# A transformer layer's two attentions: fill matmuls in pieces of six behind groups of transposes, and another order of units, loads and buffers

## The chip, the cores and the metric

The kernel runs on one core of a Trainium2 chip. The metric is the device time of one execution in microseconds (us); a kernel's time is the median of its runs. The core has five engines that run their own instruction streams in order and wait for each other through semaphores: TensorE (PE: matrix products and transposes), VectorE (DVE), ScalarE (ACT), GpSimd (POOL) and SyncE (SP), which here only issues DMA transfers. ACT issues some transfers too, in its own stream between its other work.

## The reference, cut to what matters

One layer of an encoder over 2048 tokens of 1024 features, in float32:

```
h  = rms_norm(x, norm_mix);  z = h @ w_in
z  -> q_A | k_A | v_A | q_B | k_B | v_B | gate_A | gate_B
yA = windowed GQA: 8 heads in 2 key groups, blocks of 128 queries, |t-s| <= 128,
     ALiBi slopes, a sink logit per head
yB = neighbourhood attention, 8 heads: each token of a 32 x 64 grid sees 8 rows x 16 columns,
     with a learned relative bias (rpb)
merged = sigmoid(gate_A) * (yA @ w_proj_a) + sigmoid(gate_B) * (yB @ w_proj_b)
x  = x + merged @ w_out
x  = x + relu(rms_norm(x) @ w_up)^2 @ w_down;   out = rms_norm(x)
```

## The kernel before, in words

Every float32 operand of a matmul is split into a rounded part and a remainder, and a product is made of three matmuls (`mm3`, L201: high by high, high by low, low by high), each 128x512. The stages run one after the other: the norm and the input projection (to about 535 us), attention A (to about 830 us), attention B (to about 1171 us), then the second projection, `w_out` and the MLP. This change touches only the two attentions; the streams of the later stages are the same in both kernels.

**Attention A** (`attn_a`, L829) has 32 units, one for each key group `g` and block `i` of 128 queries. A unit has two halves. The first makes the scores: for each of four heads two matmuls into a PSUM tile `s` (L844/845; three such tiles take turns), bias and maximum on DVE (L846), exponential on ACT (L853), sums on DVE, and the normalisation on POOL (L857). The second half has three groups (two at the ends of the sequence). A group is four PE transposes into a PSUM tile `pt` (L863; two such tiles), a rounded copy on ACT (`ph`, L866), the remainder on DVE (`pl`, L867), and two matmuls that add to the PSUM tile `av` (L868/869). There is one `av` tile, so the next unit's first `av` matmul waits until ACT and DVE have taken the unit's result out into `ya` (L872/873).

**Attention B** (`attn_b`, L1011) has 32 units, 8 heads by 4 column tiles, of the same two halves: scores (L1029), bias and maximum on DVE into `sb`/`stb` (L1034), exponential (L1040), normalisation on POOL (L1045), then four groups of three or four transposes (L1057), `phb` (L1062), `plb` (L1063), and `av` matmuls (L1068); `yb` takes the result out (L1076/1077). The bias tables `biass` and `biasl` of a head are made on POOL (L997) from `braw` and from `masks`, which are loaded once (L979, 1.6 MB). A head's keys `kb` are 2 MB in three transfers (`load_k`, L1006 to 1008), a unit's queries `qb` 256 KB (L1016).

**The fill.** Both attentions have PE wait for other engines, so other matmuls stand between their parts: the gates of two token pages (`gate_tile`, 16 tiles, each with two runs of 24 matmuls into a PSUM tile `mm`, whose result `z` ACT stores to `zg`), and then, in attention B, the projection of `yA` (`proj_tile`, 8 tiles of 48 matmuls). The latter needs pages of `yA` that are loaded back from memory and split on ACT (L282) and DVE (L283), in `y_page`. `chain` runs these generators one after the other and starts the loads of weights two tiles ahead. `paced` says how early a piece of fill may stand: its n-th piece, a run of 24 (or, in a projection tile, of 48), is put with `tc.issue_after` behind the last `av` matmul of one unit, kept in `done`. That sets an order on PE only and makes no engine wait; Tile's scheduler makes the streams of the engines from it. `drive` runs the units, with the first halves two units ahead of the second.

**Buffers.** `pools` opens the SBUF buffers of a stage on the left or right side, in the order of its list. A buffer of attention B that lies where one of attention A lay can be loaded only when A's last reader is through: the list decides what a load waits for.

## Time and profile before

| | us |
|---|---|
| runs of the kernel before | 2677.56, 2681.48, 2682.59 |
| their median | 2681.48 |
| the profiled execution's own time | 2674.47 |
| its span in the profile | 2672.7 |
| PE busy in the span | 2578.7 (96%) |
| DVE, ACT, POOL busy | 1703.9, 1308.6, 335.3 |
| mean granted PE clock | 0.987 |

The rows of the profile have these forms. A window gives, for a stretch of time, each engine's busy time with the number of its instructions, the granted clock of PE as a share of full speed, the share of the DMA engines that is busy, and GB/s. A wait gives the instruction that stood, what released it, and the total, the number and the longest of such waits. A row of the timeline gives an instruction's start, its duration, its line and tiles, and in brackets the idle time of its engine just before it, with what ended it. A matmul's duration overlaps the next one's, so that two starts tell what one costs, and PE's busy time counts no moment twice. The span is 1.8 us shorter than the execution's own time, and that is 7.0 us shorter than the median of the three runs.

### The profile page before, as it was taken

The page shows a single profiled execution, that of the slowest core. Times are in us where ns is not written, and L with a number is a line of the kernel's source. Part 1 is how long each engine was busy: PE and PEld are TensorE (multiplying, and loading weights), DVE is VectorE, ACT ScalarE, POOL GpSimd, SP SyncE. Part 2 cuts the span into 40 slices and gives each one's busy share as a digit, 9 for nine tenths or more (in the row PEclk, how much of TensorE's full clock was granted, in tenths as well). Part 3 has the DMA queues.
Part 4 walks back from the last instruction along what each step waited for, and adds up shares of the span by engine and source line. Part 5 has one row for each costly group of instructions (what it writes and reads, how often), then busy time and mean ns, then how long its engine had stood idle before and what let it go on. Part 6 is the DMA issues. An engine that isn't in the chain of part 4 may idle for free. (4 is left out here: it accounts for less than half of the span.)

```text
span 2672.7 us, 34547 instructions
## 1 busy us (share of the span) xinstructions
PE 2578.7 (96%) x11936; PEld 2127.9 (80%) x11936; DVE 1703.9 (64%) x2700; ACT 1308.6 (49%) x2349; POOL 335.3 (13%) x460
## 2 busy tenths in 40 slices
PE   7999999989997989999999999999999999999998
PEld 6887888877876877888877888888887888888887
DVE  7756576646663566656597766776566634555667
ACT  7365465547664665532435555554444232332444
POOL 1001001033333644300000000000000000000011
PEclk9999999989998999999999999999999999999999
DMA  5778478873337798769798655864436935445555
GB/s 181 228 197 284 147 274 262 258 222 88 95 87 198 199 255 248 215 211 345 252 339 261 237 208 199 280 222 147 150 115 245 325 123 177 148 145 169 184 186 174
DMA packets 348159, 553.21 MB, mean 207 GB/s; under 512 B 30904, under 2 KB 152888, under 8 KB 345808
## 3 DMA queue, kind: packets, MB, share of 16 engines
q1 hardware_dynamic: 328912, 506.96, 58.9%
q10 hardware_dynamic: 15552, 32.51, 3.3%
q0 software_dynamic: 3520, 11.54, 1.2%
q8 instruction: 94, 1.54, 0.2%
q14 instruction: 81, 0.66, 0.1%
HBM read 364.19 MB, written 186.71 MB: 206 GB/s over the span
## 5 line engine op out<-in xcount | busy, mean ns | idle before, releaser
L287 PE MATMUL b<-dwh,dah 128*128 128x512 f32 x896 | 348.9, 389 | 0.4 <-DVE dwh L283 0.4
L288 PE MATMUL b<-dwh,dah 128*128 128x512 f32 x896 | 348.0, 389 | 0.0
L286 PE MATMUL b<-dwh,dah 128*128 128x512 f32 x896 | 338.5, 389 | 1.7 <-ACT dwh L282 1.7
L282 ACT CAST dah<-da 128x1024 fp32r<-128x1024 f32 (+1 forms) x128 | 120.8, 944 | 367.4 <-PE b L288 245.1
L286 PE MATMUL zb<-zh,zwhl 128*128 128x512 f32 x728 | 285.8, 393 | 7.9 <-ACT zb L532 2.4
L288 PE MATMUL zb<-zh,zwhl 128*128 128x512 f32 x728 | 283.8, 391 | 1.2 <-DVE zwhl L283 1.2
L287 PE MATMUL zb<-zh,zwhl 128*128 128x512 f32 x728 | 284.8, 391 | 0.0
L283 DVE TENSOR_TENSOR dah<-da,dah 128x1024 fp32r<-128x1024 f32 (+1 forms) x128 | 139.3, 1090 | 218.4 <-ACT dah L282 213.9
L286 PE MATMUL b<-ubh,uwhlb 128*128 128x512 f32 x592 | 231.7, 391 | 5.0 <-ACT uwhlb L282 3.4
L287 PE MATMUL b<-ubh,uwhlb 128*128 128x512 f32 x592 | 231.3, 391 | 0.0
L288 PE MATMUL b<-ubh,uwhlb 128*128 128x512 f32 x592 | 229.4, 390 | 0.0
L286 PEld LDWEIGHTS b<-dwh,dah 128*128 128x128 f32 x896 | 168.1, 188 | 36.9 <-ACT dwh L282 2.1
L287 PEld LDWEIGHTS b<-dwh,dah 128*128 128x128 f32 x896 | 168.2, 188 | 35.7 <-DVE dwh L283 0.8
L288 PEld LDWEIGHTS b<-dwh,dah 128*128 128x128 f32 x896 | 168.2, 188 | 34.9
L279 DVE TENSOR_TENSOR uc<-b,uc 128x512 f32<-128x512 f32 x160 | 109.3, 689 | 117.3 <-PE b L288 111.1
L286 PEld LDWEIGHTS zb<-zh,zwhl 128*128 128x128 f32 x728 | 136.7, 188 | 41.6 <-ACT zb L532 3.9
L288 PEld LDWEIGHTS zb<-zh,zwhl 128*128 128x128 f32 x728 | 136.8, 188 | 30.8 <-DVE zwhl L283 2.7
L287 PEld LDWEIGHTS zb<-zh,zwhl 128*128 128x128 f32 x728 | 136.8, 188 | 27.4
L202 PE MATMUL mm<-zh,whl 128*128 128x512 f32 x384 | 156.0, 406 | 0.6 <-ACT zh L282 0.6
L204 PE MATMUL mm<-zh,whl 128*128 128x512 f32 x384 | 151.6, 395 | 0.0
L203 PE MATMUL mm<-zh,whl 128*128 128x512 f32 x384 | 150.7, 392 | 0.3 <-DVE zh L283 0.3
L286 PEld LDWEIGHTS b<-ubh,uwhlb 128*128 128x128 f32 x592 | 111.6, 189 | 29.2 <-ACT uwhlb L282 3.8
(249 smaller groups left out, 5689.0 us busy)
## 6 DMA issues: line engine op xcount, KB each, us to landing
at<-uc SPq DMA_DIRECT2D x224, 256.0 KB, 2.1
da<-at SPq DMA_DIRECT2D x96, 512.0 KB, 3.5
dw<-in_w_down_dram SPq DMA_DIRECT2D x160, 256.0 KB, 5.0
uraw<-in_w_up_dram SPq DMA_DIRECT2D x32, 1024.0 KB, 7.7
pgl<-wo_d SPq DMA_DIRECT2D x28, 1024.0 KB, 8.5
zraw<-in_w_in_dram SPq DMA_DIRECT2D x24, 1024.0 KB, 8.9
z<-zg SPq DMA_DIRECT2D x64, 256.0 KB, 4.9
qs_a<-ze SPq DMA_DIRECT2D x32, 256.0 KB, 3.2
```

The lines of the kernel that those rows point to most:

```text
L202: PE.matmul(ps, lh, rh, start=first, stop=False)
L203: PE.matmul(ps, lh, rl, start=False, stop=False)
L204: PE.matmul(ps, ll, rh, start=False, stop=last)
L279: return eng.tensor_tensor(out=out, in0=a, in1=b, op=op).ins
L282: A.copy(hi, src)
L283: return eng.tensor_tensor(out=lo, in0=src, in1=hi.bitcast(F32), op=ALU.subtract).ins
L286: PE.matmul(ps, lh, rh, start=first, stop=False, skip_group_check=True)
L287: PE.matmul(ps, lh, rl, start=False, stop=False, skip_group_check=True)
L288: PE.matmul(ps, ll, rh, start=False, stop=last, skip_group_check=True)
```

## The change

Four things are changed together.

1. The fill comes in pieces of six matmuls. `gate_tiles` and `in_chunks` stop after each two of the eight `mm3`, and `proj_tile` after each two of four. The last two gate tiles are made together, page 3 before page 2. `marks` takes the place of `done`: it keeps the last transpose of each group (92 in A, 128 in B). `paced` puts piece number `given` behind mark `given*(span+lag)//(total-tail)-lag`. Attention A is given 84 pieces (504 matmuls, 528 before), attention B 108 (648, 624 before).
2. A's units run in another order: group 1 blocks 0 to 4, all of group 0, then group 1 blocks 5 to 15 (before: all of group 1, then all of group 0).
3. A's keys and values, in four halves of 1.5 MB, were all loaded before the first unit. Now the first half stands there, the second behind two units, and the other two behind the sixth unit's queries. `dist` is loaded first.
4. The buffers of A have other places: `biasa1`, `ka1` and `va1` lie on the left, and `dist`, `sta`, `qa` first; only `biasa0`, `va0`, `ka0` are left on the right, where B's masks, `qb`, `braw0` and first `biass` begin. `y_page` takes other pages of the input ring: (6, 3, 1, 2) in place of (1, 2, 6, 3).

The core of the diff:

```diff
-    ap_ = pools(s_a, "left", ("ka1", "va1", "qa", "sta", "sa", "ya", "dist", "ph", "pl"), "a")
-    ap_.update(pools(s_a, "right", ("biasa0", "va0", "ka0", "biasa1"), "a"))
+    ap_ = pools(s_a, "left", ("dist", "sta", "qa", "biasa1", "ka1", "va1", "sa", "ya", "ph", "pl"), "a")
+    ap_.update(pools(s_a, "right", ("biasa0", "va0", "ka0"), "a"))
...
-                PE.transpose(pt[:, h * P : (h + 1) * P], s[:, h, c * P : (c + 1) * P], ident)
+                last = PE.transpose(pt[:, h * P : (h + 1) * P], s[:, h, c * P : (c + 1) * P], ident).ins
+            marks.append(last)
...
-    def paced(filler, pieces, total, lag):
-        for n in pieces:
-            at = min(n * 32 // total - lag, 31)
-            with tc.issue_after(done[at]) if at >= 0 else nullcontext():
-                next(filler, None)
+    def paced(filler, given, total, span, lag, tail=0, last=False):
+        while given[0] < total:
+            at = given[0] * (span + lag) // (total - tail) - lag
+            if at >= len(marks):
+                if not last:
+                    return
+                at = len(marks) - 1
+            with tc.issue_after(marks[at]) if at >= 0 else nullcontext():
+                next(filler)
+            given[0] += 1
+    def in_chunks(ps, hl, pages):
+        hi, lo = pages
+        for k in range(KC):
+            mm3(ps, hl[:, 0, k, :], hl[:, 1, k, :], hi[k // 4][:, k % 4, :], lo[k // 4][:, k % 4, :],
+                k == 0, k == KC - 1)
+            if k % 2 and k < KC - 1:
+                yield
...
-        hi, lo = (in_page[(1, 2, 6, 3)[b]]() for _ in range(2))
+        hi, lo = (in_page[(6, 3, 1, 2)[b]]() for _ in range(2))
...
                     mm3(ps, hl[:, 0, c, :], hl[:, 1, c, :], hi[:, c], lo[:, c], c == 0, c == 3)
+                    if c == 1:
+                        yield
...
-    fill = [gate_tile(f, (2, 3)) for f in range(16)] + [proj_tile(f) for f in range(8)]
+    fill = [gate_tiles(f) for f in range(14)] + [gate_tiles(14, 15)] + [proj_tile(f) for f in range(8)]
...
     load_kv(1, 0)
-    load_kv(1, 1)
+    drive((attn_a(g, i) for g, i in units_a[:2]), live, False)
     load_kv(0, 0)
-    load_kv(0, 1)
-    drive((attn_a(1, i) for i in range(14)), live, False)
-    paced(fill, range(11), 22, 3)
...
+    drive((attn_a(g, i) for g, i in units_a[2:8]), live, False)
+    with tc.issue_after(began[5]):
+        load_kv(0, 1)
+        load_kv(1, 1)
+    drive((attn_a(g, i) for g, i in units_a[8:14]), live, False)
+    paced(fill, given, 84, 92, 12)
...
-    paced(fill, range(11), 21, 3)
+    given = [0]
+    paced(fill, given, 108, 128, 4, 10)
```

Three places in the streams show what it moves. The first is SP at the start of attention A. `ka1`, `va1` are the keys and values of group 1 and `ka0`, `va0` those of group 0; `ks_a0` and `ks_a1` are the two halves of the sequence; `qa` are a unit's queries. Before, from the second half of group 1's keys on:

```order
L824 DMA ka1_476_4520<-ks_a1_81 128x1024
L825 DMA ka1_476_4520<-ks_a1_81 64x1024
L826 DMA ka1_476_4520<-ks_a1_81 64x1024
L827 DMA va1_478_4522<-vs_a1_83 128x1024
L824 DMA ka0_475_4519<-ks_a0_80 128x1024
L825 DMA ka0_475_4519<-ks_a0_80 64x1024
L826 DMA ka0_475_4519<-ks_a0_80 64x1024
L827 DMA va0_477_4521<-vs_a0_82 128x1024
L824 DMA ka0_475_4519<-ks_a1_81 128x1024
L825 DMA ka0_475_4519<-ks_a1_81 64x1024
L826 DMA ka0_475_4519<-ks_a1_81 64x1024
L827 DMA va0_477_4521<-vs_a1_83 128x1024
```

At the same row of SP's stream the changed kernel has:

```order
L824 DMA ka0_475_4519<-ks_a0_80 128x1024
L825 DMA ka0_475_4519<-ks_a0_80 64x1024
L826 DMA ka0_475_4519<-ks_a0_80 64x1024
L827 DMA va0_477_4521<-vs_a0_82 128x1024
L837 DMA qa_498_4671<-qs_a10_78 128x4x128
L189 DMA raw_618_5634<-in_w_in_dram 128x8x128
L837 DMA qa_508_4742<-qs_a10_78 128x4x128
L837 DMA qa_519_4818<-qs_a00_76 128x4x128
L824 DMA ka0_475_4519<-ks_a1_81 128x1024
L825 DMA ka0_475_4519<-ks_a1_81 64x1024
L826 DMA ka0_475_4519<-ks_a1_81 64x1024
L827 DMA va0_477_4521<-vs_a1_83 128x1024
```

The first 1.5 MB (group 1, first half) stand ahead of both pieces. Three halves followed in one run; now one follows, and the queries of three units and a tile of weights stand ahead of the next.

The second place is SP where A ends and B begins. `masks`, `braw` and `qb` are B's; the first `y_a<-ya` row of a piece is the store of A's last unit but one, the second that of the last unit. Before:

```order
L175 DMA y_a0_142<-ya_813_7090 64x4x128
L979 DMA masks_841_7523<-in_mask_b_dram 128x3200
L1016 DMA qb_845_7535<-qs_b0_84 128x4x128
L1016 DMA qb_848_7543<-qs_b0_84 128x4x128
L175 DMA y_a0_142<-ya_818_7117 64x4x128
L991 DMA braw1_856_7579<-tab1_153 128x1x512
L1016 DMA qb_857_7584<-qs_b0_84 128x4x128
```

And in the changed kernel:

```order
L175 DMA y_a1_143<-ya_809_7042 64x4x128
L1012 DMA braw1_855_7551<-tab1_153 128x1x512
L1027 DMA kb0_841_7497<-ks_b0_88 128x2048
L1028 DMA kb0_841_7497<-ks_b0_88 64x2048
L175 DMA y_a1_143<-ya_814_7069 64x4x128
L1029 DMA kb0_841_7497<-ks_b0_88 64x2048
L1040 DMA vb1_857_7558<-vs_b0_92 96x4x256
```

`masks` and the first `qb` have moved ahead, 25 rows up among A's stores, to where the last unit of group 0 is through. `kb0`, the first head's keys, stood 13 rows ahead of `masks` before; now its first transfer waits for the last `av` matmul of A, and its third stands behind the store of A's last unit.

The third place is PE in the middle of attention B. `pt` is the target of a group's transposes, `av` the sum of a unit, and `mm` the fill. Before, around the last group of one unit and the first of the next:

```order
L1057 MATMUL pt_7976<-ident,sb_887_7735 128x128
L1057 MATMUL pt_7976<-ident,sb_888_7740 128x128 x2
L1068 MATMUL av_7937<-plb_7969,vb_883_7719 128x256
L1068 MATMUL av_7937<-phb_7968,vb_883_7719 128x256
L1068 MATMUL av_7937<-plb_7969,vb_883_7719 128x256
L1057 MATMUL pt_8033<-ident,sb_902_7820 96x128 x2
L1057 MATMUL pt_8033<-ident,sb_903_7825 96x128
L1068 MATMUL av_7937<-phb_7980,vb_883_7719 128x256
```

In the changed kernel, two groups on in the same stage:

```order
L1078 MATMUL pt_8224<-ident,sb_934_7981 128x128
L1078 MATMUL pt_8224<-ident,sb_935_7986 128x128 x2
L1078 MATMUL pt_8224<-ident,sb_936_7991 128x128
L202 MATMUL mm_8973<-zh_297_2862,whl_8906 128x512
L203 MATMUL mm_8973<-zh_298_2863,whl_8906 128x512
L204 MATMUL mm_8973<-zh_297_2862,whl_8906 128x512
L202 MATMUL mm_8973<-zh_297_2862,whl_8906 128x512
L203 MATMUL mm_8973<-zh_298_2863,whl_8906 128x512
L204 MATMUL mm_8973<-zh_297_2862,whl_8906 128x512
L1090 MATMUL av_8198<-phb_8203,vb_931_7970 128x256
L1090 MATMUL av_8198<-plb_8204,vb_931_7970 128x256
```

Before, the group `pt_7976` is followed by three `av` matmuls and three transposes, and then by its own `av` (`phb_7980` is the copy of `pt_7976`). After, a piece of six fill matmuls stands between a group's transposes and the next `av` matmuls, which moreover belong to an earlier group.

More of the change, by code (lines that the diff above doesn't have):

```diff
@@ L868, in attn_a @@
             PE.matmul(po, v[:, i - 1 + c, :], ph, start=c == c0, stop=False)
-            last = PE.matmul(po, v[:, i - 1 + c, :], pl, start=False, stop=c == c1 - 1).ins
-        done.append(last)
+            PE.matmul(po, v[:, i - 1 + c, :], pl, start=False, stop=c == c1 - 1)
         t = T(ap_, [64, 512], F32, "ya", 2)
@@ L955, in encoder_layer @@
     make_bias_a(1)
[L957 removed]
+    live, given = [], [0]
+    units_a = [(1, i) for i in range(5)] + [(0, i) for i in range(16)] + [(1, i) for i in range(5, 16)]
     load_kv(1, 0)
[L959 removed]
+    drive((attn_a(g, i) for g, i in units_a[:2]), live, False)
     load_kv(0, 0)
[L961 to L966 removed]
+    drive((attn_a(g, i) for g, i in units_a[2:8]), live, False)
[4 more added lines that the diff above has]
+    paced(fill, given, 84, 92, 12)
+    drive((attn_a(g, i) for g, i in units_a[14:]), live, True)
+    paced(fill, given, 84, 92, 12, last=True)
+    del marks[:]
     flush(queue=SY)
@@ L1056, in attn_b @@
                     rr = (4 * c - B_R0[i]) * w
-                    PE.transpose(pt[:kp, at + (i - i0) * P : at + (i - i0 + 1) * P], s[i][:, rr : rr + kp], ident)
+                    last = PE.transpose(pt[:kp, at + (i - i0) * P : at + (i - i0 + 1) * P], s[i][:, rr : rr + kp], ident)
                 pieces.append((c, i0, ni, at))
                 at += ni * P
+            marks.append(last.ins)
             ph = T(bp, [P, 512], F32R, "phb", 3)
@@ L1131, in encoder_layer @@
         next_y = next(first_y)
-    paced(fill, range(11, 26), 21, 3)
+    paced(fill, given, 108, 128, 4, 10, True)
     flush(queue=SY)
```

34 lines of the change are left out of this document (15 added, 19 removed).

## The prediction

> **What bounds the kernel now.** I read the page first, for the engine that is hardly ever idle.
>
> ```profile
> PE 2578.7 (96%) x11936; PEld 2127.9 (80%) x11936; DVE 1703.9 (64%) x2700; ACT 1308.6 (49%) x2349; POOL 335.3 (13%) x460
> ```
>
> PE is idle for 2672.7 − 2578.7 = 94.0 us. The PE work is the same in both kernels (504 + 648 fill matmuls after, 528 + 624 before; the rest only changes its order), so the change can win only idle time of PE and time at a clock below 1. Next I read the windows, for where these lie; after each window come its length, the busy time of the five engines (PE first), PE's granted clock, the DMA share and GB/s.
>
> ```profile
> 560.00:600.00 40.00, 31.11 (x150) 26.02 (x149) 21.81 (x68) 22.90 (x66) 14.48 (x21) 0.83 0.65 176
> 600.00:650.00 50.00, 48.95 (x248) 38.85 (x248) 32.19 (x94) 37.12 (x100) 19.07 (x28) 1.00 0.33 95
> 650.00:700.00 50.00, 48.72 (x249) 38.20 (x248) 31.27 (x95) 32.74 (x90) 17.57 (x26) 1.00 0.30 85
> 700.00:750.00 50.00, 49.71 (x261) 41.75 (x260) 31.02 (x87) 34.07 (x90) 20.49 (x30) 1.00 0.36 98
> 750.00:800.00 50.00, 49.03 (x256) 40.38 (x255) 31.68 (x93) 34.89 (x92) 18.54 (x27) 1.00 0.29 80
> 800.00:835.00 35.00, 28.39 (x143) 22.52 (x141) 12.66 (x26) 15.21 (x32) 6.60 (x6) 0.96 0.70 206
> 835.00:860.00 25.00, 16.47 (x57) 13.51 (x58) 8.96 (x29) 7.80 (x23) 12.58 (x14) 0.58 0.74 196
> 860.00:900.00 40.00, 38.03 (x220) 31.64 (x219) 22.14 (x61) 26.11 (x67) 31.85 (x39) 1.00 0.70 186
> 900.00:950.00 50.00, 47.82 (x296) 41.20 (x296) 29.75 (x80) 33.60 (x88) 30.70 (x38) 1.00 0.85 220
> 950.00:1000.00 50.00, 41.36 (x222) 33.71 (x221) 30.86 (x64) 28.24 (x63) 21.31 (x25) 0.93 0.88 251
> 1000.00:1050.00 50.00, 45.49 (x271) 38.19 (x270) 33.52 (x83) 30.00 (x79) 22.40 (x30) 1.00 0.90 256
> 1050.00:1100.00 50.00, 47.52 (x285) 41.88 (x283) 33.52 (x83) 28.02 (x73) 25.39 (x33) 0.97 0.84 237
> 1100.00:1150.00 50.00, 45.62 (x265) 39.59 (x265) 32.58 (x79) 29.20 (x76) 16.66 (x27) 0.93 0.64 194
> 1150.00:1180.00 30.00, 29.42 (x156) 25.32 (x155) 13.44 (x21) 8.32 (x15) 0.00 (x0) 0.95 0.42 130
> 1250.00:2672.00 1422.00, 1401.84 (x6158) 1156.69 (x6156) 918.46 (x1207) 619.36 (x922) 23.39 (x33) 1.00 0.59 205
> ```
>
> I count as lost, in each window, the idle time plus the busy time multiplied by (1 − clock). That gives 14.2 us at the start of attention A (560 to 600: 8.9 idle, 5.3 slow), 3.6 in 600 to 800, 23.1 at the join of A and B (7.7 in 800 to 835, 15.4 in 835 to 860), and 33.7 in the rest of B (24.7 idle and 9.0 slow). That is 74.6 us in all, and no more than that can be won. The last row holds the later stages, which the change leaves alone.
>
> Third come PE's waits, for the causes: first in A (535 to 835), then in B (835 to 1180). Each row has the total, the number of waits and the longest.
>
> ```profile
> PE av L868 <- ACT ph L866: 8.1, 2, 7.7
> PE av L868 <- DVE ya L873: 3.2, 7, 0.9
> ```
>
> ```profile
> PE av L1068 <- DVE yb L1077: 8.8, 6, 2.4
> PE s L1029 <- DMA qb<-qs_b: 7.8, 1, 7.8
> PE s L1029 <- DVE stb L1034: 5.6, 9, 2.1
> PE pt L1057 <- DVE plb L1063: 5.2, 6, 1.8
> PE av L1068 <- DVE plb L1063: 4.0, 7, 1.1
> PE pt L1057 <- POOL sb L1045: 3.2, 1, 3.2
> PE av L1068 <- ACT phb L1062: 1.9, 3, 1.4
> ```
>
> A has one long wait, and B has one long wait at the join and many short ones for DVE and ACT. DVE is at most about two thirds busy in these windows. So it is no bound by throughput; PE meets it too early.
>
> **The change part by part.**
>
> *Start of A (order of loads).* The 7.7 us wait, in the timelines of PE and ACT, with two windows behind it and a group of DVE:
>
> ```profile
> 570.87 0.79 PE L868 MATMUL av<-ph,va 128*128 128x512 f32 x1 [7.68 <-ACT ph L866]
> 566.95 0.20 ACT L849 ACTIVATE sta<-sta 128x4 f32<-128x4 f32 x1 [8.82 <-DMA ka<-ks_a]
> ...
> 571.00:576.00 5.00, 3.95 (x12) 2.62 (x12) 1.14 (x2) 3.00 (x11) 1.62 (x3) 0.50 1.10 307
> 576.00:581.00 5.00, 4.84 (x20) 4.37 (x21) 3.98 (x12) 2.36 (x6) 2.27 (x4) 0.63 0.58 161
> ...
> L846 DVE CUSTOM_DVE_ANT_0 sa<-s,biasa,sink_t 128x384 f32<-128x384 f32 (+1 forms) x99 | 55.6, 598 | 37.7 <-PE pt L863 30.2 <-PE s L845 7.4
> ```
>
> ACT stood for a load of keys (in its stream the issue of a `zg` store comes first, and that waits for the load), PE for ACT. Three 1.5 MB halves are loaded here in one run, with the DMA engines full (share 1.10). The change puts two halves behind the sixth unit's queries, so this wait should go. What is late next is DVE: the new order has 26 score matmuls in a run, 13 pairs. PE starts a matmul of 512 columns every 1401.84/6158 = 0.23 us (last window above), so a pair of 384 columns takes about 2 × 0.75 × 0.23 = 0.35 us; DVE's operation on it takes 0.60 (its group in 600 to 800, the last row). So the run takes 13 × 0.25 = 3.2 us longer than its matmuls, and about 1.3 more, an estimate, until POOL has the first unit. That makes 4.5 idle, 2 slow (of 3.95 × 0.50 + 4.84 × 0.37 = 3.8 slow now) and 1.3 of small waits as now: 7.8 for 14.2, a gain of **6.4**. Bounds: 0 if another load takes the wait over, 11 if only the small waits and some slow time stay.
>
> At this place a rule of the page can be weighed, beside the two windows: after the wait the clock is below 1 for about 9 us. The Trainium skill (TensorE: Matmul & The Clock Gate, Part 1, "What's actually happening") says that PE's clock is halved after an idle window of about 3.4 us and full again after about 3.4 us of sustained work. By that rule alone the slow loss would be half of 3.4, about 1.7 us, an estimate from that page, and the term would be 2 us smaller; the rows show more than twice that, and the sum goes by the rows.
>
> *Middle of A.* 3.6 us are lost, most of it `ya` (3.2 us). With a piece of fill behind each group the next unit's `av` comes later. I take **1.0**; bounds 0 and 3. The masks and queries of B are loaded in this stretch now; with a DMA share of 0.29 to 0.36 there they cost nothing. Without that cover, they would cost what they cost at the join, which comes next.
>
> *The join (places of buffers).*
>
> ```profile
> 800.90 0.34 SPq L1006 DMA_DIRECT2D kb<-ks_b  x1
> ...
> 837.99 4.41 PE L1029 MATMUL s<-kb,qb 128*128 128x288 f32 x14 [7.75 <-DMA qb<-qs_b]
> 845.62 1.65 PE L1057 MATMUL pt<-ident,sb 128*96 128x128 f32 x7 [3.23 <-POOL sb L1045]
> 853.15 0.85 PE L1029 MATMUL s<-kb,qb 128*128 128x288 f32 x2 [2.12 <-DVE stb L1034]
> 858.31 0.73 PE L202 MATMUL mm<-zh,whl 128*128 128x512 f32 x1
> ...
> 830.26 0.35 SPq L979 DMA_DIRECT2D masks<-in_mask_b_dram  x1
> ...
> masks<-in_mask_b_dram SPq DMA_DIRECT2D x1, 1600.0 KB
> ```
>
> Keys went out at 800.90, long ahead. Masks and queries waited for A's last matmul, and PE stood 7.75 us; then 3.23 for POOL, whose tables need the masks, and the first fill came at 858.31. The change takes masks and queries ahead, but `kb0` takes their place: 2 MB, at the end of A, with a store of `ya` ahead of its third transfer. That is one wait for another. From 1600 KB and one `qb` in the 7.73 us from 830.26 to 837.99, 2048 KB at the same rate take 7.73 × 2048/1856 = 8.5 us. Behind it come 24 score matmuls in 12 pairs on which DVE is again the slower (12 × 0.25 = 3.0), and then some 0.2 until POOL: 11.7 idle. But behind the first transposes stands fill, so the 2.12 us wait and the slow run to 858 shrink. I put the slow time at 4.5 (16.47 × 0.42 = 6.9 now) and the end of A at 1.5. The sum is 17.7 for 23.1, a gain of **5.4**. Bounds: 0 (the new load costs what the old did) and 10 (the slow time and POOL's wait go altogether).
>
> *Rest of B (the pieces of six).* A copy on ACT and a remainder on DVE stand between a group's transposes and its `av`:
>
> ```profile
> L866 ACT CAST ph<-pt 128x512 fp32r<-128x512 f32 x71 | 40.7, 583 | 27.1 <-PE pt L863 24.8 <-DVE sta L846 1.7
> L867 DVE TENSOR_TENSOR pl<-pt,ph 128x512 fp32r<-128x512 f32 x70 | 47.6, 686 | 14.1 <-ACT ph L866 13.5
> ```
>
> That is 0.58 + 0.69 us (the groups of A; B's are the same operations on up to as many columns), with the hand-overs some 1.6, an estimate. Before, a group's transposes often have less behind them. Counting matmuls at 0.23 us for 512 columns and half for 256, 37 of 128 groups have under 1.5 us there, short by 20.8 us together of 1.6 each; after, it is 0.9 us. From the last `av` of a unit to the first of the next, every third unit had only 1.3 to 1.4 us before; now nearly all have 2.4 to 4.2, more than the eviction by ACT and DVE. So `yb` should fall from 8.8 to 2, `phb` and `plb` before `av` from 5.9 to 1, `plb` before `pt` from 5.2 to 1.5, and `stb` (3.3 of the 5.6, the rest is at the join) to 2. That leaves 6.5 and 0.9 of others, if ACT and DVE keep up. In one place they don't:
>
> ```profile
> ACT zh L282 <- DMA raw<-y_a: 14.2, 6, 6.1
> ```
>
> Where the pages of `yA` come back (950 to 1020), ACT stands 14.2 us in its stream for these loads, and PE's copies stand behind it. Pages and splits are as many after. I add 3 us of idle for that, and keep 5.5 of the 9.0 slow: 7.4 + 3 + 5.5 = 16 for 33.7, a gain of **17.7**. Bounds: 10 if only the windows outside 950 to 1050 gain (1.97 + 2.18 + 2.48 + 4.38 idle there and some slow time), 29 if all but 4.7 goes.
>
> *End of B.* In the new order 49 matmuls, before 57, stand between the last unit and the work that needs its result: 8 × 0.23 = 1.8 us less cover. I take **−0.8**; bounds −2 and 0.
>
> The sum is 6.4 + 1.0 + 5.4 + 17.7 − 0.8 = 29.7 us. Against its own time of 2674.47 us the profiled execution would be at 2644.8; carried to the median of the runs, 7.0 us higher, 2681.5 − 29.7 = **2652 us**.
>
> **The rivals.**
>
> *Only the small waits go, and the loads eat the rest.* The join's load of keys costs as much as the masks did, and `y_page` keeps ACT as late as now (the 14.2 us row, DMA shares of 0.85 to 0.90 from 900 to 1050). Then the join gives 0 and B some 6: 6.4 + 1.0 + 0 + 6 − 0.8 = 12.6, **2669 us**. For it speaks the one-for-one exchange at the join, against it that fill now stands behind the first groups.
>
> *Nearly all gaps close.* 9 at the start, 2 in A, 9 at the join, 26 in B: 46, **2635.5 us**. For it speaks the order (20.8 us of short distances become 0.9), against it the shares of DMA and ACT's wait above.
>
> *The clock.* Slower than before: small pieces of matmuls alternate with transposes all through A and B, PE never does one thing for long, and the granted clock sinks over the whole stretch. Windows 950 to 1000 and 1100 to 1150 show 0.93 over a stretch, with idle of 4 to 9 us. A clock of 0.93 over the 555 us of work after the change costs 555 × (1/0.93 − 1) = 42 us, less the 30 gained: **2693 us**. It decides from a mean clock of 555/(555 + 30) = 0.95 down. Against it, 600 to 800 and 860 to 950 hold transposes, scores and fill in turn at 1.00, and fewer waits should lift the clock. Two sections of the Trainium skill's page TensorE: Matmul & The Clock Gate speak for it: Part 4, "PE-mode transpose", says that transposes do not count as busy for the clock in the same way, and "A second HAM failure mode: psum-queue depth-cycling" that small pauses between groups of matmuls can make the clock go back and forth. The windows at 1.00 do not bear that out so far.
>
> That the change doesn't do what it says is no rival of its own: the new order has its pieces of six behind the groups, and the transfers moved. What ACT and DVE do at those places is the first rival.
>
> **How the numbers follow.** The forecast (2640 to 2661) has 0.42, nearly all gaps 0.20, loads eat the rest (to 2676) 0.22, the clock 0.11, and 0.05 is left for a stall that I do not see, on the slower side. The bounds of the terms sum to 53 (11 + 3 + 10 + 29 + 0) and 8 (0 + 0 + 0 + 10 − 2): 2628 to 2674, and I take 2628 to 2675; it leaves out the clock and the unseen stall. A measurement of this kernel can tell 0.2%, 5.4 us, from no change. Faster by more is the forecast, the second rival and 0.20 of the first, 0.82; the rest of the first and a mild clock make within 0.2% 0.05; slower is 0.13.
>
> **What would show it.** At the start of A no wait of over 4 us, and none of ACT for keys; at the join one wait of 8 to 9 us for `kb` in the place of `qb`, none for masks; in B waits on `yb` of 2 us and on `phb` and `plb` of 3 together, with clocks of 1.00. Wrong would be: clocks of 0.95 or less in the middle of A or B (the clock), PE's waits in B of over 20 us behind ACT's wait for `y_a` (loads), or waits on `kb` of over 11 us.

## The result, and the profile after

The changed kernel takes **2661.48 us** in the median of five runs (2656.76 to 2668.97), the kernel before 2681.35 (2669.62 to 2682.59, five runs). The ratio is 0.9937, with a 95% interval of 0.9909 to 0.9965: some 17 us faster. The profiled execution took 2657.30 us, 17.2 less than the 2674.47 of before. The prediction was 2652, in a range of 2628 to 2675. So sign and range were right, but the gain is little more than half of the 29.7 us forecast, one term has the wrong sign, and the time lies at the upper edge of the forecast's own interval (2640 to 2661), where that of the first rival begins.

The page's first row after:

```profile
PE 2561.9 (96%) x11936; PEld 2124.7 (80%) x11936; DVE 1703.8 (64%) x2700; ACT 1308.3 (49%) x2349; POOL 336.8 (13%) x460
```

The span is 2655.5 us, so PE is idle for 93.6 us; before it was 94.0. **The idle time did not fall; PE's busy time did, by 16.8 us, for the same 11936 instructions.** How that can be is told below. First the windows of the changed kernel, in the columns of the prediction:

```profile
560.00:600.00 40.00, 34.61 (x182) 30.11 (x183) 23.26 (x77) 27.20 (x81) 17.44 (x29) 0.91 0.71 191
600.00:650.00 50.00, 48.66 (x255) 40.02 (x254) 34.32 (x101) 35.48 (x94) 18.36 (x26) 1.00 0.34 93
650.00:700.00 50.00, 48.26 (x263) 40.90 (x262) 34.46 (x94) 35.51 (x96) 20.64 (x30) 1.00 0.34 90
700.00:750.00 50.00, 49.54 (x258) 40.33 (x257) 36.35 (x100) 36.49 (x99) 22.25 (x33) 1.00 0.51 146
750.00:800.00 50.00, 47.70 (x250) 39.17 (x249) 29.21 (x75) 31.22 (x81) 19.67 (x26) 1.00 0.31 88
800.00:835.00 35.00, 17.28 (x78) 13.24 (x77) 10.68 (x31) 9.03 (x24) 8.21 (x9) 0.71 0.76 156
835.00:860.00 25.00, 19.71 (x112) 17.25 (x110) 9.70 (x30) 13.03 (x35) 17.05 (x21) 0.93 0.74 178
860.00:900.00 40.00, 40.00 (x248) 35.72 (x247) 22.81 (x64) 28.94 (x73) 28.40 (x33) 1.00 0.88 233
900.00:950.00 50.00, 49.93 (x313) 44.54 (x312) 30.66 (x80) 31.85 (x81) 25.65 (x33) 1.00 0.75 197
950.00:1000.00 50.00, 41.43 (x226) 34.12 (x224) 29.13 (x66) 30.64 (x73) 21.53 (x27) 0.90 0.86 237
1000.00:1050.00 50.00, 44.27 (x249) 38.10 (x248) 31.52 (x71) 25.66 (x64) 24.53 (x28) 0.93 0.88 248
1050.00:1100.00 50.00, 50.00 (x313) 44.97 (x311) 36.01 (x92) 29.64 (x79) 26.51 (x36) 1.00 0.80 227
1100.00:1150.00 50.00, 49.70 (x310) 43.79 (x309) 33.84 (x72) 28.66 (x70) 9.47 (x16) 1.00 0.79 245
1150.00:1180.00 30.00, 26.18 (x111) 21.13 (x110) 11.17 (x17) 5.58 (x8) 0.00 (x0) 0.94 0.74 248
```

Three places stand out. In 860 to 950 and 1050 to 1150 PE is idle for 0.4 us in all now, where it was for 2 to 4 us a window before. In 950 to 1050 14.3 us are still idle. And 800 to 835 is worse: 17.7 us idle, and a clock of 0.71. PE's waits say why, first from 535 to 840, then from 860 to 1150:

```profile
PE s L1050 <- DMA kb<-ks_b: 16.0, 2, 11.8
PE s L844 <- DMA qa<-qs_a: 5.9, 1, 5.9
PE av L869 <- DVE ya L873: 5.8, 5, 1.9
```

```profile
PE mm L202 <- ACT zh L282: 7.3, 2, 3.8
PE s L1050 <- DVE stb L1055: 2.4, 3, 1.0
PE av L1090 <- ACT phb L1084: 2.0, 1, 2.0
PE mm L203 <- DVE zh L283: 1.5, 2, 1.0
PE av L1090 <- DVE yb L1098: 0.8, 1, 0.8
PE av L1090 <- DVE plb L1085: 0.3, 1, 0.3
```

Most of the short waits of B are gone. In the same window before, 860 to 1150, `yb` had 8.8 us and `plb` before `av` 3.5; now they have 0.8 and 0.3. `phb` (1.9 before) and `stb` (3.3 before) changed little. At the join stands a wait of 16.0 us for `kb`, in the place of 7.8 for `qb`. The timelines of PE and SP there:

```profile
810.19 0.40 PE L870 MATMUL av<-pl,va 128*128 128x512 f32 x1
822.34 1.25 PE L1050 MATMUL s<-kb,qb 128*128 128x288 f32 x3 [11.75 <-DMA kb<-ks_b]
827.87 6.08 PE L1050 MATMUL s<-kb,qb 128*128 128x288 f32 x21 [4.29 <-DMA kb<-ks_b]
834.15 1.09 PE L1078 MATMUL pt<-ident,sb 128*96 128x128 f32 x6 [0.20 <-POOL sb L1066]
845.66 2.71 PE L1050 MATMUL s<-kb,qb 128*128 128x384 f32 x6 [5.29 <-DMA qb<-qs_b]
```

```profile
810.82 0.34 SPq L1027 DMA_DIRECT2D kb<-ks_b  x1
...
812.59 0.72 SPq L1029 DMA_DIRECT2D kb<-ks_b  x1
824.53 0.34 SPq L1027 DMA_DIRECT2D kb<-ks_b  x1
```

The order of the steps is the one forecast: last `av` of A, keys issued, two waits, scores, and then POOL is no wait any more. But the keys take 11.5 us from their issue to the first score and 15.3 us from the third transfer's issue to the rest (812.59 to 827.87), where 8.5 was forecast. Then the keys of the second head (824.53) are ahead of a unit's queries, and PE waits 5.3 us for those.

**Where the busy time went.** A matmul of 512 columns has a duration of 0.39 us in the records, but the next one starts 0.23 us later. So a wait of up to 0.16 us behind it lies under its duration and isn't idle time, and what runs at half clock isn't idle either. To count these too, I took the starts of PE's successive matmuls and called lost what an interval has beyond the shortest usual one (the tenth percentile) for the same pair of kinds, over all traces of this study. The sums depend on how finely the kinds are told apart; the differences between kernels hardly do (by about 1 us). Summed by stages, in us:

| | ahead of the fill | A | join | B | behind B | all |
|---|---|---|---|---|---|---|
| before | 36.6 | 41.7 | 14.6 | 80.9 | 23.6 | 197.4 |
| after | 35.4 | 35.4 | 20.8 | 58.2 | 30.6 | 180.4 |
| pieces alone | 39.6 | 32.3 | 16.0 | 58.5 | 26.8 | 173.2 |
| order and places alone | 37.3 | 37.0 | 21.3 | 75.9 | 30.5 | 202.0 |
| keys of B early | 36.4 | 33.7 | 3.7 | 54.2 | 27.2 | 155.2 |
| six behind units | 35.1 | 30.6 | 15.4 | 55.9 | 28.5 | 165.5 |
| pieces of three | 36.9 | 28.9 | 21.5 | 52.3 | 27.9 | 167.5 |
| pieces of twelve | 36.6 | 41.9 | 19.8 | 62.7 | 28.5 | 189.5 |

("Join" is from A's last `av` to B's first, B from there to its last.) The sum of after is 17.0 less than that of before, as the times are. In B, 80.9 became 58.2: 7.0 of that is idle time (27.0 to 20.0), 7.6 half clock (16.2 to 8.6), and 8.1 short intervals at full clock that no idle column shows (37.7 to 29.6). The first column is the same code in all kernels and the last nearly so; from trace to trace they differ by some 5 us, so a single difference of that size in one trace says nothing by itself.

### The profile page after: what moved, and what is told of

It is laid out like the page before. It is cut to its first block, busy times and chain, and to the rows that moved or that the text cites. A ratio compares the mean times of both kernels' runs of the same rounds, so it can differ in the third digit from the quotient of the medians.

```text
span 2655.5 us, 34541 instructions
## 1 busy us (share of the span) xinstructions
PE 2561.9 (96%) x11936; PEld 2124.7 (80%) x11936; DVE 1703.8 (64%) x2700; ACT 1308.3 (49%) x2349; POOL 336.8 (13%) x460
## 5 line engine op out<-in xcount | busy, mean ns | idle before, releaser
L286 PEld LDWEIGHTS b<-dwh,dah 128*128 128x128 f32 x896 | 168.1, 188 | 36.9 <-ACT dwh L282 2.1
L202 PE MATMUL mm<-zh,whl 128*128 128x512 f32 x384 | 165.8, 432 | 7.3 <-ACT zh L282 7.3
L288 PEld LDWEIGHTS zb<-zh,zwhl 128*128 128x128 f32 x728 | 137.0, 188 | 29.7 <-DVE zwhl L283 1.7
L203 PE MATMUL mm<-zh,whl 128*128 128x512 f32 x384 | 152.3, 397 | 1.5 <-DVE zh L283 1.5
L204 PE MATMUL mm<-zh,whl 128*128 128x512 f32 x384 | 152.4, 397 | 0.0
```

The lines of the kernel that those rows point to most:

```text
L202: PE.matmul(ps, lh, rh, start=first, stop=False)
L203: PE.matmul(ps, lh, rl, start=False, stop=False)
L204: PE.matmul(ps, ll, rh, start=False, stop=last)
L286: PE.matmul(ps, lh, rh, start=first, stop=False, skip_group_check=True)
L288: PE.matmul(ps, ll, rh, start=False, stop=last, skip_group_check=True)
```

## The experiments

My theory was that the gain in B comes from the pieces of six, because they stand behind the groups of transposes, and that the loss at the join comes from the place of B's first keys. The rivals were that order, loads and places make the gain, that the transfers are slow wherever they stand, and that it is the size of the pieces, not their place.

**Pieces alone.** The main loop, the lists of pools and the input pages of before; the fill of after:

```diff
-    units_a = [(1, i) for i in range(5)] + [(0, i) for i in range(16)] + [(1, i) for i in range(5, 16)]
+    units_a = [(1, i) for i in range(16)] + [(0, i) for i in range(16)]
...
-    ap_.update(pools(s_a, "right", ("biasa0", "va0", "ka0"), "a"))
+    ap_.update(pools(s_a, "right", ("biasa0", "va0", "ka0", "biasa1"), "a"))
```

> The fill in pieces of six behind groups of transposes, with the order of units, the loads, the places of buffers and the input pages as before. If the pieces make the gain in attention B, its short waits go as in the changed kernel (yb 8.8 to about 1 us, phb and plb before av 5.9 to about 2), the long wait of attention A's start for ACT (7.7 us) and the join's for qb (7.8 us) stay, and there is no wait for kb: about 2681 - 22 + 3 = 2662 us. If the places and loads make it, the short waits of B stay at over 15 us and the time is within 4 us of before, 2681.

Measured: **2650.8 us**, ratio to before 0.9904 (0.9889 to 0.9920). PE's waits from 535 to 1200:

```profile
PE av L869 <- ACT ph L867: 8.8, 1, 8.8
PE pt L1075 <- POOL sb L1063: 8.0, 3, 3.1
PE s L1047 <- DMA qb<-qs_b: 7.6, 1, 7.6
...
PE av L1087 <- DVE yb L1095: 0.3, 1, 0.3
```

The long waits of before are both here (8.8 for ACT at A's start, 7.6 for `qb`), and `yb` is gone. The pieces alone give all of the gain, and about 9 us more than the whole change (0.9904 against 0.9937; the intervals just overlap). In B they lose 58.5 us, as after; that the time is 11 us under my 2662 comes mostly from A (41.7 to 32.3), where I had counted nothing for them.

**Order, loads and places alone**, with runs of 24 behind units:

```diff
-    ap_ = pools(s_a, "left", ("ka1", "va1", "qa", "sta", "sa", "ya", "dist", "ph", "pl"), "a")
-    ap_.update(pools(s_a, "right", ("biasa0", "va0", "ka0", "biasa1"), "a"))
+    ap_ = pools(s_a, "left", ("dist", "sta", "qa", "biasa1", "ka1", "va1", "sa", "ya", "ph", "pl"), "a")
+    ap_.update(pools(s_a, "right", ("biasa0", "va0", "ka0"), "a"))
...
-    load_kv(1, 1)
+    drive((attn_a(g, i) for g, i in units_a[:2]), live, False)
```

> The order of units, the loads, the places of buffers and the input pages as after, with the fill in runs of 24 behind units as before. If the pieces make the gain and the places cost at the join, the wait for kb is there with over 12 us, the one for qb of 7.8 us is gone, the start of A has gained some 5 us, and the short waits of B are those of before: about 2681 - 5 + 6 = 2682 us. If the places make the gain, 2662 us.

Measured: **2676.7 us**, ratio 0.9997 (0.9987 to 1.0008), no change. PE's waits from 535 to 1200:

```profile
PE s L1033 <- DMA kb<-ks_b: 15.7, 2, 11.6
PE av L1072 <- DVE yb L1081: 8.7, 8, 2.4
PE s L1033 <- DMA qb<-qs_b: 7.6, 1, 7.6
```

The wait for `kb` is that of the changed kernel and `yb` that of before. My expectation had the wait for `qb` gone, but it is there with 7.6 us: it comes later now, behind the second head's keys. By the table A gains 4.7, the join loses 6.7 and B gains 5.0; none of these stands far above what two traces differ by.

**Keys of B early.** The changed kernel, with the left list in another order:

```diff
-    ap_ = pools(s_a, "left", ("dist", "sta", "qa", "biasa1", "ka1", "va1", "sa", "ya", "ph", "pl"), "a")
+    ap_ = pools(s_a, "left", ("sta", "ka1", "va1", "sa", "ya", "ph", "pl", "biasa1", "qa", "dist"), "a")
```

> The changed kernel, with the left side's list of attention A in an order that lets the first head's keys of B lie where the queries and bias lay, so that their load waits for A's last score matmul in place of its last av matmul, 130 PE instructions earlier. If the join is lost to that load alone, the wait for kb (16.0 us) falls under 3, and with it goes most of the half clock behind it: about 2661 - 14 = 2647 us. If the transfers are slow because they crowd each other, the wait moves to qb, the bias tables or the weights of the fill and at most 4 us are won: 2657 us or more.

Measured: **2636.8 us**, ratio 0.9845 (0.9828 to 0.9862), the fastest of the study and about 25 us under the changed kernel. PE's waits from 780 to 850, and the window of the join:

```profile
PE av L1090 <- DMA vb<-vs_b: 3.2, 1, 3.2
PE s L1050 <- DMA kb<-ks_b: 1.0, 1, 1.0
```

```profile
800.00:835.00 35.00, 31.77 (x170) 27.15 (x169) 15.79 (x45) 21.57 (x54) 20.57 (x24) 0.95 0.80 225
```

Busy time in 800 to 835 is 31.8 us, 17.3 after. The issues of the first and third transfer on SP, and the scores on PE that need them:

```profile
783.01 0.34 SPq L1027 DMA_DIRECT2D kb<-ks_b  x1
...
784.01 0.59 SPq L1029 DMA_DIRECT2D kb<-ks_b  x1
```

```profile
789.66 0.65 PE L1050 MATMUL s<-kb,qb 128*128 128x288 f32 x3
...
794.03 0.73 PE L1050 MATMUL s<-kb,qb 128*128 128x288 f32 x3 [0.99 <-DMA kb<-ks_b]
```

Two things help here. The keys start while PE has A's last units and fill to do; the first scores of B stand 124 instructions ahead of A's last `av`. And the transfers take less time: at most 6.7 us from the first issue to the first score and 10.0 from the third issue to the rest, where after had 11.5 and 15.3. At 15.3 the rest would have come 5.3 us later than it did. In the changed kernel two loads of `vb` are issued right behind the keys (813.35), in this run only at 811.53, long after them; whether they slow the keys was not tried, so the second theory, that transfers crowd each other, is not ruled out as a part of the cause. The join's 20.8 us become 3.7, a gain of 17.1 where I expected 14; the half clock behind it goes too. The other 8 us of the 25 are spread over A, B and what is behind B, in pieces under 5 us.

**The load at the end of B.** After the last unit, ACT waits 13.5 us for `yraw` in the changed kernel and PE 3.7 for ACT. From the waits of ACT (860 to 1180) and of PE (840 to 1180):

```profile
ACT pgr L1147 <- DMA yraw<-y_b: 15.2, 2, 13.5
```

```profile
PE b L202 <- ACT pgr L1147: 3.8, 2, 3.7
```

The first load of `w_out`'s pages (1 MB) had moved ahead of `yraw`. The edit puts it back:

```diff
-                SY.dma_start(raw, y_b[c][:, (2 * m + j) * BT : (2 * m + j + 1) * BT])
+                y_loads.append(SY.dma_start(raw, y_b[c][:, (2 * m + j) * BT : (2 * m + j + 1) * BT]).ins)
...
-            SY.dma_start(w.bitcast(F32), wo_d[n][h].rearrange("k p z c -> p k z c"))
+            with tc.issue_after(y_loads[7]):
+                SY.dma_start(w.bitcast(F32), wo_d[n][h].rearrange("k p z c -> p k z c"))
```

> The changed kernel, with the first load of w_out's pages (1 MB, pgl) put behind the loads of yB's first two pages (yraw) instead of ahead of them; PE's order is the same. If that load is what makes the end of B late, ACT's wait for yraw falls from 13.5 us to 9 or less and PE's wait of 3.7 us for pgr goes: about 2661 - 4 = 2657 us, and it shows in the windows from 1150 to 1250. If the fill that is left there (16 matmuls where 48 stood) is the cause, PE's wait stays at 3 us or more and the time is the same.

Measured: **2664.5 us**, ratio 0.9949 (0.9936 to 0.9962). PE's wait for `pgr` fell from 3.8 to 0.9 us, and the time did not follow, against both theories: the wait went, and nothing was gained. What is behind B loses 29.8 us for 30.6.

**More fill kept for the end of B.**

```diff
-    paced(fill, given, 108, 128, 4, 10)
+    paced(fill, given, 108, 128, 4, 18)
```

> The changed kernel, with 18 in place of 10 pieces of fill kept for behind the last unit of B (52 matmuls stand there in place of 16), and so 8 pieces fewer among its groups. The first load of w_out's pages also comes behind yraw in this order. If the end of B lacks fill, PE's wait for pgr (3.8 us) and the half clock behind it go and the time falls by 4 to 6 us, to about 2656. If the pieces are worth more among the groups than at the end, the short waits of B rise by as much and the time stays within 2 us of the changed kernel.

Measured: **2672.8 us**, ratio 0.9975 (0.9961 to 0.9989), some 10 us slower than after, though the intervals just overlap; neither theory had that. PE's waits from 535 to 1220:

```profile
PE av L1090 <- DVE yb L1098: 10.4, 3, 8.9
```

Behind B 3 us are won (27.4 for 30.6), and among the units, with 48 fill matmuls fewer, 9 are lost (66.9 for 58.2). The longest wait, 8.9 us, stands at 991 us, where the pages of `yA` come back: ACT had stood 8.4 us for them until 987.9.

**Both** the early keys and the 18 pieces:

```diff
-    ap_ = pools(s_a, "left", ("dist", "sta", "qa", "biasa1", "ka1", "va1", "sa", "ya", "ph", "pl"), "a")
+    ap_ = pools(s_a, "left", ("sta", "ka1", "va1", "sa", "ya", "ph", "pl", "biasa1", "qa", "dist"), "a")
...
-    paced(fill, given, 108, 128, 4, 10)
+    paced(fill, given, 108, 128, 4, 18)
```

> The run with the keys of B early (2637 us) and the 18 pieces kept for the end of B together. If the two places are independent, the time is 2637 - 4 = 2633 us and the windows from 1120 on show no wait over 2 us for pgr; if the end of B only passes its wait on, 2637 us.

Measured: **2639.3 us**, ratio 0.9850 (0.9829 to 0.9870): no better than the early keys alone. None of the three edits at the end of B won time.

**Pieces of twelve.**

```diff
-            if k % 2 and k < KC - 1:
+            if k == 3:
...
-    paced(fill, given, 84, 92, 12)
+    paced(fill, given, 42, 92, 12)
...
-    paced(fill, given, 108, 128, 4, 10)
+    paced(fill, given, 54, 128, 4, 5)
```

> The changed kernel with pieces of twelve matmuls behind every second mark, the same fill in all. If every group of transposes needs a piece behind it, about half of B's gain goes (the waits for phb, plb and yb rise from 3 us by 5 or more and the time by about 10, to 2672 us). If it is enough that the fill is spread evenly over a unit, the time stays within 3 us of 2661.

Measured: **2667.0 us**, ratio 0.9957 (0.9943 to 0.9971), between the two theories and, by its interval, not to be told from the changed kernel. B's waits of `av` for `yb`, `phb` and `plb` did not come back (1.8 us), but short intervals at full clock did (36.4 us in B, 29.6 after), and in A a wait that the pieces of six hardly have (0.4 us). From 600 to 800:

```profile
PE pt L863 <- DVE pl L868: 6.0, 3, 2.1
```

**Pieces of three.**

```diff
-            if k % 2 and k < KC - 1:
+            if k < KC - 1:
...
-    paced(fill, given, 84, 92, 12)
+    paced(fill, given, 168, 92, 12)
...
-    paced(fill, given, 108, 128, 4, 10)
+    paced(fill, given, 216, 128, 4, 20)
```

> The changed kernel with pieces of three matmuls, twice as many, behind the same marks: nearly every group has three or six behind it. If what counts is that no group stands bare, B loses less in short waits than with six, and the time falls by 2 to 6 us, to about 2657. If a turn between transposes and fill has a cost of its own, or the half clock comes with finer pieces, it rises over 2665.

Measured: **2642.8 us**, ratio 0.9876 (0.9857 to 0.9896), clearly faster than six, and by more than the 2 to 6 us I expected. A loses 28.9 us and B 52.3, the least in the table; the join is as bad as after. In A the wait of `av` for `ya`, 5.8 us after, is nearly gone. From 535 to 1220:

```profile
PE av L869 <- DVE ya L873: 0.5, 1, 0.5
```

Turns between transposes and fill cost nothing that shows.

**Pieces of six behind units,** not behind groups (A's edit; B's is alike):

```diff
-            marks.append(last)
...
-            PE.matmul(po, v[:, i - 1 + c, :], pl, start=False, stop=c == c1 - 1)
+            last = PE.matmul(po, v[:, i - 1 + c, :], pl, start=False, stop=c == c1 - 1).ins
+        marks.append(last)
...
-    paced(fill, given, 84, 92, 12)
+    paced(fill, given, 84, 32, 4)
...
-    paced(fill, given, 108, 128, 4, 10)
+    paced(fill, given, 108, 32, 1, 10)
```

> The changed kernel with its pieces of six put behind the last av matmul of a unit (32 places) in place of the last transpose of a group (92 and 128 places); three or so pieces share a place. If the place behind the transposes makes the gain in B, the waits for yb, phb and plb come back to 10 us or more and the time rises by about 10, to 2671 us. If it is the size of the pieces, which the scheduler can spread by itself, the time stays within 4 us of 2661.

Measured: **2644.3 us**, ratio 0.9873 (0.9859 to 0.9886), faster than the changed kernel. PE's waits from 860 to 1140:

```profile
PE mm L202 <- ACT zh L282: 6.3, 3, 3.8
...
PE av L1089 <- DVE plb L1084: 1.7, 4, 0.9
...
```

No `yb` is left. **My theory on the place falls**: the marks are not what closes the gaps. Against the run with order and places alone, which has runs of 24 behind units, little but the size differs (24 matmuls of fill stand in B instead of A): 0.9873 for 0.9997, and 55.9 us lost in B for 75.9. With pieces small enough, the scheduler puts them between the parts by itself. In A `av` waits for `ya` in after (5.8 us) and not here. The marks alone don't make that wait: pieces alone, with the same marks, has none from 600 to 800, where after has 4.4 us. The largest other difference is the join, where its order happens to leave 18 fill matmuls between A's last `av` and B's first scores, so that the wait for `kb` is 10.0 us.

**A's queries ahead of 1.5 MB.** PE's wait of 5.9 us at the start of A is for the fourth unit's queries. It is in PE's timeline, and in SP's:

```profile
565.39 0.66 PE L844 MATMUL s<-ka,qa 128*128 128x384 f32 x1 [5.94 <-DMA qa<-qs_a]
```

```profile
549.75 1.69 SPq L824 DMA_DIRECT2D ka<-ks_a  x1
...
555.47 0.55 SPq L837 DMA_DIRECT2D qa<-qs_a  x1
```

The queries leave when the first unit's scores free a buffer, and the load of keys is ahead of them. The edit puts it behind:

```diff
-    drive((attn_a(g, i) for g, i in units_a[:2]), live, False)
-    load_kv(0, 0)
+    drive((attn_a(g, i) for g, i in units_a[:4]), live, False)
+    with tc.issue_after(began[3]):
+        load_kv(0, 0)
...
```

> The changed kernel, with the load of the second half of keys and values (group 0, 1.5 MB) put behind the queries of A's fourth unit instead of ahead of them. If PE's wait of 5.9 us for those queries is their place behind 1.5 MB in the queue, it falls under 2 us and the time by about 5, to 2656 us. If the queries are late because their buffer comes free late and the DMA engines are full with other loads, the wait stays over 4 us or moves to the keys of group 0, and the time does not change.

Measured: **2659.4 us**, ratio 0.9924 (0.9906 to 0.9942). The wait fell to 2.1 us, and A loses 32.7 for 35.4, less than two traces differ by; the time is not to be told from that of the changed kernel.

**Both places mended**, keys of B early and queries of A first:

```diff
-    ap_ = pools(s_a, "left", ("dist", "sta", "qa", "biasa1", "ka1", "va1", "sa", "ya", "ph", "pl"), "a")
+    ap_ = pools(s_a, "left", ("sta", "ka1", "va1", "sa", "ya", "ph", "pl", "biasa1", "qa", "dist"), "a")
...
+    with tc.issue_after(began[3]):
+        load_kv(0, 0)
```

> The two places mended: B's first keys loaded behind A's last scores, and the second half of A's keys and values behind the queries of the fourth unit. If both stand apart, 2637 - 2 = 2635 us, with no wait over 2.5 us before 940 us.

Measured: **2645.5 us**, ratio 0.9862 (0.9838 to 0.9885). That is not apart from the early keys alone (0.9845), and 10 us over what I expected. Two waits over 2.5 us are left ahead of 940 us, 4.0 for `vb` at the join and 3.0 for queries. Its profiled execution lost 45.5 us ahead of the fill, in code that is the same in all kernels, so its parts say nothing against the sum.

**Pages of yA earlier,** on top of both:

```diff
         raw = load_slice([(cols(w_pa[0], f * P), 4)])
+        if f == 0:
+            y_page(0)
+            y_page(1)
         yield
```

> The kernel with both places mended, and with the first two pages of yA loaded and split one tile of fill earlier than the projection needs them. If ACT's wait for these loads is what makes PE wait in the middle of B (PE's matmuls waited 12 us for ACT's split of zh in the run with the keys early), that wait falls under 5 us and the time by about 6, to 2629 us. If the DMA engines are simply full there, the wait only moves to other loads: within 2 us of 2635.

Measured: **2640.7 us**, ratio 0.9860 (0.9843 to 0.9876), no change. The wait of `mm` for `zh` is gone; another one stands in its place. PE's waits from 535 to 1220:

```profile
PE s L1054 <- DVE stb L1059: 8.3, 4, 5.8
```

DVE itself stands ahead of that, for 8.75 us. Its timeline:

```profile
968.81 0.69 DVE L965 SCALAR_TENSOR_TENSOR z<-z,mm 128x512 f32<-128x512 f32 x1 [8.75 <-issue]
```

The instruction needs the gates `z`, loaded from `zg` with issues at 954.56 and 959.32, and the share of the DMA engines in 960 to 968.8 is 1.06. The trace names no releaser, so that it is this load is my reading; it is what the second theory has, by which the wait only moves to other loads.

## Why the prediction was right and where it was not

The premise of the sum was that only idle time of PE and time at half clock can be won. It does not hold: by that measure the windows of 560 to 1180 lost 74.6 us before and lose 71.0 after, so 3.6 of the 17 us show there; A and the rest of B lose less by it, the join and the end of B more. Much of the gain lies under the matmuls' durations, where the sum did not look.

*Rest of B, 17.7 us forecast: right in the causes, in size only by another measure.* The short waits were to fall to 6.5 us and are 5.5 (`stb`, `phb`, `yb` and `plb` in the second list of waits). By the starts of matmuls B loses 22.7 less. But the sum had left 16 us of idle and slow time from 860 on, and the windows to 1150 alone have 21.9 (31.7 before). That 22.7 comes near 17.7 is in part luck. Two things were off. The pages of yA were to cost 3 us of new idle time and cost 8.8 (7.3 + 1.5 against 0.6 + 0.3 before), though the idle time of 950 to 1050 rose only from 13.2 to 14.3: PE seems to come to them earlier and to wait where before it was late itself, which was not tried. And part of the gain was not in the idle time and clock that I summed: 8.1 us were short intervals under the matmuls' durations. My reason, "pieces of fill stand behind the groups", was the wrong half of the edit: six behind units does as well, and 24 behind units do not, so the size is what counts; of three sizes behind groups the smallest was the fastest.

*The join, +5.4 forecast: wrong, it is −6.2* (20.8 for 14.6 in the table; 29.4 for 23.1 by the windows). The step that failed is "2048 KB at the same rate take 8.5 us". The rate was that of the masks, another transfer. The page of before had the keys' own time, in the list of transfers with the median from issue to landing:

```profile
kb<-ks_b SPq DMA_DIRECT2D x8, 1024.0 KB, 6.6
kb<-ks_b SPq DMA_DIRECT2D x16, 512.0 KB, 9.6
```

The halves of 512 KB are issued up to 0.9 us behind the 1024 KB of the same keys, so 9.6 us is about what a whole set of 2 MB took, and the nearer row to take. Yet it would not have been enough: with 9.6 in place of 8.5 the term is still +4.3. The waits for the keys became 16.0 us, a sign of being wrong that I had named (over 11). The DMA engines moved 200 GB/s from 811 to 822.3 with a share of 0.94, where they had moved 323 with a share of 1.00 for the masks (830.2 to 838 before). What held the rate down (`braw` and `vb` are loaded beside the keys) was not tried. The step from the 17.7 us I had left at the join to 29.4 is made up of 7.5 for the keys, 5.3 for the queries behind the second head's keys, which the sum does not hold, and 1.9 more slow time, less the 3.0 for DVE, which did not come. I had the mechanism, the exchange of one wait for another, and its place, but not its size. The first rival had this exchange at 0, and the truth is beyond it. The run with the early keys shows that the order of one list made it: 17.1 us come back at the join.

*Start of A, +6.4: 5.7 by the windows* (8.5 for 14.2 in 560 to 600), for another reason. ACT's wait for keys went, as forecast, but not DVE and POOL came next: the next load did, queries behind 1.5 MB (5.9 us, where I had said no wait over 4).

*Middle of A, +1.0: −2.2 by the windows.* Idle time in 600 to 800 is 5.8 us for 3.6, with `ya` still the cause. Six behind units has no such wait from 600 to 795, but neither has pieces alone, with the same marks and the old order of units; what brings marks and `ya` together was not tried. By the starts of matmuls A as a whole gains 6.3 all the same.

*End of B, −0.8: not settled.* PE waits 3.7 us there and did not before, though by the count of matmuls only 8 fewer stand ahead, and mending it won nothing. The kernel with order and places alone, which has the fill at the end as before, loses 30.5 us behind B, as after does.

*The clock, at 0.11, did not come.* The mean granted clock is 0.988 for 0.987, and the windows of 600 to 800 stand at 1.00 in both kernels. The sign I had named for it, 0.95 or less in the middle of B, is there in two windows, 0.90 and 0.93 in 950 to 1050 (0.93 and 1.00 before); but there PE waits for the pages of `yA`, and the windows on both sides, with the same mixture of work, have 1.00. The price of this rival stands on 555 us of work, which no row gives; in the windows of 560 to 1180 PE is busy for 567.6 us before, which makes it 43 in place of 42.

The Trainium skill's page TensorE: Matmul & The Clock Gate says in Part 4, "PE-mode transpose", that transposes don't count as busy for the clock in the same way; the rows at 1.00 show no cost of that here.

In both kernels the trace's record of the clock has stretches at half clock of 3.41 us or a multiple in the attentions. The Trainium skill's page TensorE: Matmul & The Clock Gate, Part 1, "What's actually happening", has a window of about 3.4 us; the unit agrees. I had set 9 us against that rule, too quickly. From the first matmul behind a wait to full clock it took 3.8 us after the wait of 5.9 (565.39 to 569.16), 4.1 after the last wait for `kb` at the join (827.87 to 831.99), and 8.8 only after the wait of 7.7 before (570.87 to 579.70), where PE stood for 1.2 us more on the way.

So the sum was 29.7 us, and 17.2 came. By the table the parts are 6.3 in A (7.4 forecast), −6.2 at the join (5.4), 22.7 in B (17.7), −7.0 behind B (−0.8) and 1.2 ahead of the fill, where nothing was changed. The join is the error that counts, 11.6 us, and what is behind B the next, 6.2, of which a part can be the spread between traces. B's excess of 5.0 made up for some of it, so that the time came into the range is partly luck. It lies 9.5 us from the forecast of 2652 and 7.5 from the 2669 of the first rival, "only the small waits go, and the loads eat the rest"; for the join that rival was the better account, for the short waits of B the forecast was.

## What to carry to other kernels

Fill between dependent steps should be offered in small pieces; how small mattered more here than the place they were tied to. When buffers change places, ask of each first load of the next stage what it now waits for, and price it by that transfer's own time from issue to landing, among the loads that will stand beside it, not by another's rate. Count what lies under the matmuls' durations too, by their starts, or the sum misses part of the gain. A wait mended where another stands close behind may give nothing: three of the mended waits here (for the load at the end of B, A's queries and yA's pages) moved the time by less than could be told.

## What the runs showed of the hardware that I had not expected

- PE's idle time was 94.0 us before and 93.6 after, with 17 us between the times: waits shorter than the 0.16 us by which a matmul's recorded duration exceeds the distance of starts count as busy.
- Bytes alone did not tell how long a load takes: with 1.6 MB of masks and a unit's queries PE started 7.7 us after the first issue; with 2 MB of keys, in three transfers, 11.5 us after it, and 15.3 us after the third transfer's issue for what needed all. In the run with the early keys, issued some 28 us sooner, the same two times were at most 6.7 and 10.0 us. A key transfer of 512 KB took longer in the median (9.6 us) than one of 1024 KB (6.6 us); it is issued behind the latter, by 0.4 to 0.9 us for the first head before, and whether anything else adds to it was not tried.
- Code that is the same in all kernels, ahead of the fill, took 540.0 to 550.8 us in 14 traces. So a difference under some 5 us between two traces is no effect by itself.
